# A triangular inverse that keeps its running matrix in PSUM, and a new static order around it

## The chip, the cores and the metric

One core of one Trainium2 chip runs the whole program. The metric is the device time of one execution in microseconds (us). All times below are in us unless marked ns. TensorE is called PE (its weight loads PEld), VectorE DVE, ScalarE ACT, GpSimd POOL, and SyncE, which issues most DMAs, SP.

## The reference

One layer of a hybrid decoder for two request groups that share weights: 1024 prompt tokens and 8 decode tokens. Each token passes a half-step SwiGLU network, a mixing layer and a second half-step SwiGLU network:

```python
h = x + 0.5 * rmsnorm(swiglu(rmsnorm(x, lp['n_ffn1_pre']), lp['ffn1_gate'], lp['ffn1_up'],
                             lp['ffn1_down']), lp['n_ffn1_post'])
u = rmsnorm(h, lp['n_mix_pre'])
proj = u @ lp['w_in']
...
mix = jnp.concatenate([ya, yb], axis=-1) @ lp['w_out']
h = h + rmsnorm(mix, lp['n_mix_post'])
h = h + 0.5 * rmsnorm(swiglu(rmsnorm(h, lp['n_ffn2_pre']), lp['ffn2_gate'], lp['ffn2_up'],
                             lp['ffn2_down']), lp['n_ffn2_post'])
```

`ya` is differential attention of 4 heads, `yb` an RWKV-7 recurrence of 8 heads with a 64 x 64 state each:

```python
def step(s, inp):
    r_t, w_t, k_t, v_t, kk_t, a_t = inp
    sa = jnp.einsum('nhvk,nhk->nhv', s, -kk_t)
    s = (s * w_t[:, :, None, :] + sa[..., None] * (kk_t * a_t)[:, :, None, :]
         + v_t[..., None] * k_t[:, :, None, :])
    return s, jnp.einsum('nhvk,nhk->nhv', s, r_t)
```

The kernel does this recurrence in chunks of 64 tokens. Inside a chunk it needs the inverse of a triangular matrix, and that inverse is what the change touches.

## The kernel before

**Halves and phases.** The tokens are cut into two halves of 512 (one carries the 8 decode tokens too). The two networks on two halves make four phases: phase 0 and 1 are the first network on half 0 and 1, phase 2 and 3 the second network. All their gate, up and down matmuls come from one stream, `s_trunk`, named `trunk`. Weights are loaded in full precision and split into two rounded parts (ACT rounds, DVE or POOL subtracts: `wts_w` for the trunk, `lin_w` for the projections), and each product takes three matmuls. Phases 1 and 2 use matmuls of 512 columns (wide) except for their last tiles; the others use 256 or 264 (narrow). A phase ends with its tail: norm, residual, and for phases 0 and 1 the normed input of the mixing projection (`tail_xl`, `tail_T`). The tail of phase 2 is named `last`, the end of phase 3 `end`.

**Mixing of one half.** `proj_m` computes the projection `w_in`. Four jobs (`s_job`, function `job`) do two RWKV heads each, jobs 0 and 2 on buffer set 0, jobs 1 and 3 on set 1. Attention (`attn`, with `prep` before and `fin` after each head) follows. Then `s_out` multiplies by `w_out`: `out_m` for half 0, `outb_m` for half 1, 384 matmuls each. Its norm is `s_outnorm`: one statistics matmul `outn_dec` per chunk of about 256 tokens, then additions on DVE and POOL into `out_T` or `outb_T`. After it `s_stats` and `s_pre` make the rounded input of the next network: `pre_X` for phase 2, `pre_T` for phase 3. The handover from mixing to the next network is this chain of matmul, norm, statistics and rounding. `rows` transposes half 1's residual for the output.

**One job.** It builds its operands on all engines, multiplies, and writes 32 x 32 blocks of a lower triangle to DRAM (`Md`). The inverse reads them back into `LT` (`job_LT` for set 0, `job_lraw` for set 1), laid out so that each of 128 partitions holds part of one block, and loads a starting block into `X`. Then 31 steps follow, each with two DVE instructions: a product of one row of `LT` with one column of `X` into `tm`, and an addition of `tm` onto the rest of `X`. Each needs the one before. `X` and `tm` lie in one SBUF tile, which the trace names `bset_solve` for set 0 and `job_hres` for set 1. The result goes through DRAM (`Xd`) into the matrix `TT`, and the job's later matmuls use it. A job has one PSUM bank, `aux0` or `aux1` (named `job_aux` in the trace), which `ps2()` hands out; during the inverse it is not used.

**What sets the order.** Every piece of work is a stream, a generator that hands its instructions to a queue per engine. `Kern.run` takes them one at a time, by a cost formula for each instruction (`price`), and fixes the order on each engine before the program runs; on the chip every engine executes its list in that order. [...] Of the instructions ready at about the same time the one with the smallest `late` goes first, a due time that the previous planning pass left for it (`latest`). `either` chooses between DVE and POOL (or ACT) for some instructions by what stands in their queues, so a new order also moves some work between engines. The program plans `PASSES` times and uses the pass whose own total is lowest.

Of the kernel before, what the change touches and what calls it, by code (L numbers as in the profile page):

```python
# [83 lines left out]
MW = 1  # L84
MARG = 0
SLACK = 0.02
PASSES = 10

PRIO = {"stats": (1, 1), "lin": (1, 1), "proj": (1, 1), "tail": (0, 0), "dec": (1, 1), "job": (-2, 0), "trunk": (-1, 3), "wts": (0, 0), "outb": (1, 1), "out": (0, 0), "resid": (-2, 0)}

# [93 lines left out]
class Kern:  # L184
# [97 lines left out]
    def put(self, eng, op, fn, a, k):  # L282
        st = self.cur
        outs = [a[0]] + ([k["accum_out"]] if "accum_out" in k else [])
        ins = [getattr(x, "ap", None) if isinstance(x, bass.IndirectOffsetOnAxis) else x for x in a[1:]]
        ins += [v for n, v in k.items() if n != "accum_out"]
        ins = [x for x in ins if isinstance(x, bass.AP)]
        i = len(self.ops)
        o = Op(eng, lambda: fn(*a, **k), st)  # L289

        o.key = st.key, st.count
        st.count += 1

        o.before = st.put.get(eng)
        st.put[eng] = i
        o.late = self.late.get(o.key) if self.late else None
        self.price(o, op, a, k, outs[0], ins)
        if op == "activation" and a[2] in TABLE:
            o.table = TABLE[a[2]]
        deps = set()  # L300
        for write, aps in ((False, ins), (True, outs)):
            for ap in aps:
                nm = ap.tensor.name
                if nm in self.tiles:
                    s, row = self.tiles[nm]
                    assert s.tenant == nm, (nm, s.tenant)
                    q, w = self.region(ap, s, row)
                    deps |= s.before
                    if ap.space == PSUM:

                        deps.update(j for (e, _), j in s.last.items() if e != eng)
                    s.last[eng, st] = i
                    deps.update(np.unique(s.wrote[q, w]).tolist())
                    if write:
                        for r in s.read.values():
                            deps.update(np.unique(r[q, w]).tolist())
                            r[q, w] = -1
                        s.wrote[q, w] = i
                    else:
                        if (eng, st) not in s.read:  # L320
                            s.read[eng, st] = np.full((4, s.words), -1, np.int64)
                        s.read[eng, st][q, w] = i
                elif nm in self.drams:
                    shape, seen = self.drams[nm]
                    box = self.box(ap, shape)
                    deps.update(j for b, w, j in seen if (write or w) and all(x[0] <= y[1] and y[0] <= x[1] for x, y in zip(b, box)))
                    seen.append((box, write, i))
        deps -= {-1, i}
        for j in deps:
            d = self.ops[j]  # L330
            if d.end is None:
                d.then.append(o)
                o.left += 1
            else:
                o.ready = max(o.ready, self.after(d, o))
        o.deps = deps
        self.ops.append(o)
        self.backlog[eng] += o.cost
        st.q[eng].append(o)
        st.n += 1  # L340
# [68 lines left out]
    def spawn(self, gen, label, prio, *banks, ahead=None):  # L409
        prio = PRIO.get(label.rstrip("01"), prio)  # L410
        self.streams.append(Stream(gen, label, prio, banks))
        k = self.spawned[label] = self.spawned.get(label, -1) + 1
        self.streams[-1].key = label, k
        if ahead is not None:
            self.streams[-1].ahead = ahead

# [358 lines left out]
    def s_weights(self):  # L775

        nc, I = self.nc, self.I
        groups, seq = self.plan()
        last, turn = {}, -1
        for ph in range(4):  # L780
            tags = ("w0", "w1", "w2", "w3")[:4 if ph in (0, 3) else 2]
            turn = -1
            for n, (kind, f, m0) in enumerate(seq):
                if ph == 1 and n == 2 * LEAD:
                    yield ("wait", ("loaded", ("in", 0), 25))
                    last |= {tag: ("used", ("in", 0), 24 + i) for i, tag in enumerate(tags)}
                turn += 1
                tag = tags[turn % len(tags)]
                if ph == 3 and turn == 2:
                    yield ("wait", ("outw", 1))  # L790
                raw = self.raw()
                w = I[f"ffn{1 + ph // 2}_{kind}"]
                if kind == "down":
                    grp = groups[f]
                    a = len(grp)
                    nm = self.down_tiles(grp) * P
                    raw = raw[:, :a * nm]
                    src = w[0, grp[0] * P:(grp[-1] + 1) * P, m0 * P:m0 * P + nm].rearrange("(q p) m -> p q m", p=P)
                else:
                    src, a = self.column(w, f), KT  # L800
                nc.sync.dma_start(raw.rearrange("p (a b) -> p a b", a=a), src)
                if tag in last:
                    yield ("wait", last[tag])
                self.W[ph, kind, f, m0] = self.split(raw, tag, a)
                self.signal(("loaded", ph, kind, f, m0))
                last[tag] = ("used", ph, kind, f, m0)
                yield

    def s_trunk(self):

        nc = self.nc
        V, A, G = nc.vector, nc.scalar, nc.gpsimd
        groups, _ = self.plan()
        for ph in range(4):
            if ph == 0:
                ring = self.T(self.big, [P, 4160], "xl1", FR)
            wide = ph in WIDE
# [543 lines left out]
    def job(self, pool, i, s, jb):  # L1361
# [3 lines left out]
        V, A, G = nc.vector, nc.scalar, nc.gpsimd  # L1365
# [5 lines left out]
        r, k, v = F("r"), F("k"), F("v")  # L1371
# [3 lines left out]
        ps = self.ps2()  # L1375
# [5 lines left out]
        ps = self.ps2()  # L1381
# [10 lines left out]
        ps = self.ps2()  # L1392
        for j in range(4):
            mm(ps[:, 2 * j:2 * j + 2], sq[:, j * P:(j + 1) * P], self.ind2, start=True, stop=True)
        rn, sx, st = (x[:, j] for x in [self.T(pool, [P, 3, 8], "stf")] for j in range(3))
# [7 lines left out]
        ps = self.ps2()  # L1403
# [12 lines left out]
        ps = self.ps2()  # L1416
# [33 lines left out]
        for w0 in (-1, 3, 7):  # L1450
            ps = self.ps2().rearrange("p (n h t) -> p n h t", n=4, h=2)
# [21 lines left out]
        for g in range(2):  # L1473
            for h, q in H:
                ps = self.ps2().rearrange("p (n w t) -> p n w t", n=4, w=2)
# [17 lines left out]
        for n in range(NC):  # L1493
            for h, q in H:
                o = H[1 - h][1]
# [10 lines left out]
        solve = [x[:, 256 * j:256 * j + 256] for j in range(2)]  # L1506
# [2 lines left out]
        for cg in range(4):  # L1509
            nc.sync.dma_start(LT[32 * cg:32 * cg + 32], src)  # L1510
        LT = LT.rearrange("p (s t) -> p s t", s=32)
        X, tm = (t.rearrange("p (c i) -> p c i", i=32) for t in solve)
        yield
        for j in range(31):
            w, m = 31 - j, j // 4 + 1
            V.tensor_tensor(tm[:, :m, :w], LT[:, j, j + 1:].unsqueeze(1).broadcast_to([P, m, w]),
                            X[:, :m, j:j + 1].broadcast_to([P, m, w]), ALU.mult)
            V.tensor_tensor(X[:, :m, j + 1:], X[:, :m, j + 1:], tm[:, :m, :w], ALU.add)
            if j % 2:
                yield  # L1520
        for cg in range(4):
            nc.sync.dma_start(self.Xd[jb][:, :, cg, :], X[32 * cg:32 * cg + 32])
        yield
# [9 lines left out]
        ps = self.ps2().rearrange("p (n t) -> p n t", t=C)  # L1533
# [7 lines left out]
        for g in range(2):  # L1541
            ps = self.ps2().rearrange("p (n h t) -> p n h t", n=4, h=2)
# [4 lines left out]
        ps = self.ps2().rearrange("p (n t) -> p n t", t=C)  # L1547
# [9 lines left out]
        for g in range(2):  # L1557
            ps = self.ps2().rearrange("p (n w t) -> p n w t", n=4, w=2)
# [11 lines left out]
        for g in range(2):  # L1570
            ps = self.ps2().rearrange("p (n w t) -> p n w t", n=4, w=2)
# [34 lines left out]
        st = J([P, 3, 8], "st")  # L1606
# [12 lines left out]
        ps = self.ps2()  # L1619
# [6 lines left out]
        ps = self.ps2()  # L1626
# [684 lines left out]
```

## Time and profile before

| | us |
|---|---|
| runs | 2412.41, 2413.09, 2421.26 (median 2413.09) |
| the profiled execution | 2414.15 |
| its span on the core | 2412.3 |
| from 2012 to 2412 (phase 3): PE busy | 392.68 |

The profile's page gives busy time by engine and 40 slices of the span, with the granted clock of PE in tenths. A group of instructions is a row: engine, operation, tile written and tiles read, shape, count, then busy us, mean ns of one, and the idle time of the engine just before them with what ended it. A row of a table by windows gives start and end, the length, then busy us and instructions of PE, PEld, DVE, ACT and POOL, the granted clock (1 is full), the DMA share and GB/s. Almost every row has line 289, since one helper issues all planned instructions; the tile names tell them apart. The DMA queues carry little that decides here:

```profile
q1 hardware_dynamic: 460824, 294.78, 42.5%
HBM read 254.86 MB, written 41.46 MB: 123 GB/s over the span
```

### The profile page before, as it was taken

What the parts mean: (1) busy time and instruction counts of PE and PEld (TensorE: products, weight loads), DVE (VectorE), ACT (ScalarE), POOL (GpSimd) and SP (SyncE); (2) the same over time, 40 slices, a digit from 0 to 9 for tenths busy, and PEclk for the clock granted to TensorE, in tenths of its full rate; (3) what the DMA queues carried; (4) which work ended last, traced back from release to release, by engine and by line L of the source; (5) the groups of instructions that cost most, each with busy time, mean ns of one, the idle gap of its engine ahead of it and who ended that gap; (6) DMA issues with size and microseconds to landing.
All of it is one profiled execution on the core that took longest, in us unless ns stands there. A gap on an engine that the chain in (4) does not pass through costs nothing. (4 is left out here: it accounts for less than half of the span.)

```text
span 2412.3 us, 42260 instructions
## 1 busy us (share of the span) xinstructions
PE 2306.1 (96%) x16207; PEld 2045.4 (85%) x16207; DVE 1504.6 (62%) x3057; ACT 1023.0 (42%) x2008; POOL 967.4 (40%) x767
## 2 busy tenths in 40 slices
PE   7999999999999999996899999999999987999998
PEld 6999999799977778786887776777777887999998
DVE  5554445756379778567786288586687577343444
ACT  5532223543432443366543442443466455322224
POOL 4442223533087443446574244243434365111112
PEclk9999999999999999998899999999999998999999
DMA  6423233345375345465686343233534544323232
GB/s 202 126 87 92 87 91 120 110 147 151 97 220 166 99 114 147 121 167 154 161 223 178 114 118 90 61 94 87 154 112 132 156 121 113 114 85 93 88 92 76
DMA packets 461635, 299.09 MB, mean 124 GB/s; under 512 B 81114, under 2 KB 428862, under 8 KB 461433
## 3 DMA queue, kind: packets, MB, share of 16 engines
q1 hardware_dynamic: 460824, 294.78, 42.5%
q8 instruction: 128, 2.10, 0.4%
q0 software_dynamic: 320, 1.08, 0.1%
q14 instruction: 75, 0.61, 0.1%
q10 hardware_dynamic: 288, 0.52, 0.1%
HBM read 254.86 MB, written 41.46 MB: 123 GB/s over the span
## 5 line engine op out<-in xcount | busy, mean ns | idle before, releaser
L289 PE MATMUL trunk_m<-pre_X,wts_w 128*128 128x256 f32 (+2 forms) x3264 | 545.9, 321 | 11.0 <-DVE trunk_g L289 4.4
L289 POOL TENSOR_TENSOR wts_w<-wts_raw,wts_w 128x1024 fp32r<-128x1024 f32 (+1 forms) x147 | 334.8, 2278 | 524.4 <-ACT wts_w L289 445.4
L289 PE MATMUL trunk_m<-trunk_xl,wts_w 128*128 128x256 f32 (+2 forms) x2952 | 508.4, 324 | 14.9 <-DVE trunk_xl L289 13.8
L289 PEld LDWEIGHTS trunk_m<-pre_X,wts_w 128*128 128x128 f32 x3264 | 455.1, 190 | 56.2 <-issue 7.5
L289 ACT CAST wts_w<-wts_raw 128x1024 fp32r<-128x1024 f32 (+1 forms) x288 | 281.3, 977 | 445.3 <-PE trunk_m L289 360.3
L289 PEld LDWEIGHTS trunk_m<-trunk_xl,wts_w 128*128 128x128 f32 x2952 | 420.4, 190 | 55.7 <-DVE trunk_xl L289 15.6
L289 PE MATMUL trunk_m<-pre_T,wts_w 128*128 128x256 f32 (+2 forms) x2592 | 445.7, 327 | 2.1 <-DVE wts_w L289 0.8
L289 PEld LDWEIGHTS trunk_m<-pre_T,wts_w 128*128 128x128 f32 x2592 | 375.7, 188 | 45.7 <-issue 3.7
L289 POOL TENSOR_TENSOR trunk_xl<-trunk_t,trunk_xl 128x256 fp32r<-128x256 f32 (+2 forms) x104 | 114.9, 1105 | 290.1 <-ACT trunk_xl L289 290.0
L289 DVE TENSOR_TENSOR trunk_xl<-trunk_xl,trunk_m 128x256 f32<-128x256 f32 (+2 forms) x314 | 155.8, 502 | 112.3 <-PE trunk_m L289 110.8
L289 DVE TENSOR_TENSOR wts_w<-wts_raw,wts_w 128x1024 fp32r<-128x1024 f32 (+1 forms) x141 | 162.5, 1153 | 65.3 <-ACT wts_w L289 62.8
L289 PE MATMUL proj_m<-tail_xl,lin_w 128*128 128x256 f32 (+1 forms) x832 | 159.9, 290 | 4.0 <-ACT tail_xl L289 4.0
L289 PE MATMUL proj_m<-tail_T,lin_w 128*128 128x512 f32 (+1 forms) x672 | 153.1, 384 | 0.1
L289 PEld LDWEIGHTS proj_m<-tail_T,lin_w 128*128 128x128 f32 x672 | 119.7, 190 | 26.6 <-issue 2.0
L289 PEld LDWEIGHTS proj_m<-tail_xl,lin_w 128*128 128x128 f32 x832 | 132.4, 192 | 7.4 <-ACT tail_xl L289 4.5
L289 PE MATMUL proj_m<-tail_X,lin_w 128*128 128x256 f32 (+1 forms) x416 | 121.9, 293 | 0.4 <-DVE tail_X L289 0.3
L289 ACT CAST trunk_xl<-trunk_t 128x256 fp32r<-128x256 f32 (+2 forms) x136 | 64.0, 471 | 127.2 <-DVE trunk_t L289 78.8
L289 DVE SCALAR_TENSOR_TENSOR trunk_g<-trunk_t,trunk_m 128x512 f32<-128x512 f32 (+2 forms) x78 | 43.4, 557 | 91.4 <-ACT trunk_t L289 90.8
L289 POOL TENSOR_TENSOR trunk_g<-trunk_g,init_rb 128x256 f32<-128x256 f32 (+1 forms) x44 | 42.0, 956 | 135.0 <-ACT trunk_t L289 135.0
L289 PE MATMUL trunk_aux<-pre_T,wts_w 128*128 128x264 f32 (+1 forms) x672 | 85.4, 283 | 0.0
L289 PEld LDWEIGHTS proj_m<-tail_X,lin_w 128*128 128x128 f32 x416 | 80.1, 193 | 3.9 <-issue 2.2
L289 PEld LDWEIGHTS trunk_aux<-pre_T,wts_w 128*128 128x128 f32 x672 | 82.4, 188 | 0.0
(498 smaller groups left out, 3610.7 us busy)
## 6 DMA issues: line engine op xcount, KB each, us to landing
wts_raw<-in_ffn_gate_dram SPq DMA_DIRECT2D x88, 512.0 KB
wts_raw<-in_ffn_up_dram SPq DMA_DIRECT2D x88, 512.0 KB
wts_raw<-in_ffn_down_dram SPq DMA_DIRECT2D x96, 384.0 KB
lin_raw<-in_w_in_dram SPq DMA_DIRECT2D x26, 512.0 KB
mix_T<-PT SPq DMA_DIRECT2D x37, 256.0 KB
wts_raw<-in_ffn_down_dram SPq DMA_DIRECT2D x16, 512.0 KB
dec_dreg<-in_cache_k_dram SPq DMA_DIRECT2D x32, 256.0 KB
dec_dreg<-in_cache_v_dram SPq DMA_DIRECT2D x32, 256.0 KB
```

The costliest lines, as they stand in the source:

```text
L289: o = Op(eng, lambda: fn(*a, **k), st)
```

## The change

The inverse now takes the job's own PSUM bank for `X`. ACT copies the starting block from SBUF into the bank (256 columns), the 31 steps read and write `X` there while `tm` and `LT` stay in SBUF, and ACT copies the result back, so that the DMA can read it. Each of the eight jobs has two more ACT copies. The arithmetic is the same.

The order is planned anew. A table `BIAS` adds microseconds to the due times of eight streams: negative numbers make a stream more urgent (the weights of phase 3, half 1's last job, the tail of phase 0's second chunk, the norm of half 0's first chunk), positive ones less (the residual load of phase 0, the second half's input, half 1's two norms). Streams get a name with a number for that (`part`), and the number of planning passes goes from 10 to 4.

```diff
@@ -84,7 +84,8 @@
 SLACK = 0.02
-PASSES = 10
+PASSES = 4
+BIAS = {"tail1": -10, "ldxb0": 10, "wts3": -30, "outn3": 3, "job13": -30, "outn2": 3, "resid0": 60, "outn0": -10}
@@ -294,6 +295,8 @@
         o.late = self.late.get(o.key) if self.late else None
+        if o.late is not None:
+            o.late += BIAS.get(st.part, 0)
         self.price(o, op, a, k, outs[0], ins)
@@ -411,6 +414,7 @@
         self.streams[-1].key = label, k
+        self.streams[-1].part = f"{label}{k}"
@@ -778,6 +782,7 @@
         for ph in range(4):
+            self.cur.part = f"wts{ph}"
@@ -812,6 +817,7 @@
         for ph in range(4):
+            self.cur.part = f"trunk{ph}"
@@ -1509,7 +1515,10 @@
         LT = LT.rearrange("p (s t) -> p s t", s=32)
-        X, tm = (t.rearrange("p (c i) -> p c i", i=32) for t in solve)
+        cols = lambda t: t.rearrange("p (c i) -> p c i", i=32)
+        ps = self.ps2()
+        X, tm = cols(ps[:, :256]), cols(solve[1])
+        A.copy(ps[:, :256], solve[0])
         yield
         for j in range(31):
             w, m = 31 - j, j // 4 + 1
@@ -1518,6 +1527,8 @@
             V.tensor_tensor(X[:, :m, j + 1:], X[:, :m, j + 1:], tm[:, :m, :w], ALU.add)
             if j % 2:
                 yield
+        A.copy(solve[0], ps[:, :256])
+        X, tm = (cols(t) for t in solve)
         for cg in range(4):
```

**The inverse on DVE.** The first job's inverse begins so in the list of DVE before (`bset_solve` is `X` and `tm` in SBUF):

```order
L289 TENSOR_TENSOR mix_T_580_5265<-mix_T_580_5265,mix_T_581_5266 128x512
L289 TENSOR_TENSOR bset_solve_181<-job_LT_5921,bset_solve_181 128x31
L289 TENSOR_TENSOR bset_solve_181<-bset_solve_181 128x31
L289 TENSOR_TENSOR bset_solve_181<-job_LT_5921,bset_solve_181 128x30
L289 TENSOR_TENSOR bset_solve_181<-bset_solve_181 128x30
```

And now:

```order
L290 TENSOR_TENSOR mix_T_580_5287<-mix_T_580_5287,mix_T_581_5288 128x512
L290 TENSOR_TENSOR bset_solve_181<-job_LT_5870,job_aux_641_5871 128x31
L290 TENSOR_TENSOR job_aux_641_5871<-job_aux_641_5871,bset_solve_181 128x31
L290 TENSOR_TENSOR bset_solve_181<-job_LT_5870,job_aux_641_5871 128x30
L290 TENSOR_TENSOR job_aux_641_5871<-job_aux_641_5871,bset_solve_181 128x30
```

Each product reads `X` from the bank `job_aux`, each addition reads and writes it there; one SBUF input is left in both.

**The first handover on PE** (half 0's norm, `outn_dec`, after the last `out_m`). Before, phase 1's trunk is finished, and the next half's projection follows:

```order
L289 MATMUL out_m_1337_12650<-out_X_1250_11596,lin_w_1319_12522 128x256 x2
L289 MATMUL out_m_1337_12650<-out_X_1251_11597,lin_w_1319_12522 128x256
L289 MATMUL out_m_1337_12650<-out_X_1250_11596,lin_w_1319_12522 128x256
L289 MATMUL proj_m_1367_12714<-tail_T_1296_11849,lin_w_1363_12710 128x256
L289 MATMUL outn_dec_12622<-bset_la_173,init_onesD_76 128x256
L289 MATMUL proj_m_1367_12714<-tail_T_1297_11850,lin_w_1363_12710 128x256
```

Now (`decb` is work of the decode tokens):

```order
L290 MATMUL trunk_m_1233_11509<-trunk_xl_56_153,wts_w_1227_11468 128x512 x3
L290 MATMUL decb_dec_10963<-decb_dreg_10961,bset_wa_166 128x8 x4
L290 MATMUL trunk_m_1233_11509<-trunk_xl_56_153,wts_w_1227_11468 128x512 x2
L290 MATMUL outn_dec_11971<-bset_la_173,init_onesD_76 128x256
L290 MATMUL trunk_m_1233_11509<-trunk_xl_56_153,wts_w_1227_11468 128x512 x4
L290 MATMUL trunk_m_1234_11529<-trunk_xl_56_153,wts_w_1227_11468 128x512 x9
L290 MATMUL trunk_m_1237_11547<-pre_T_132_513,wts_w_1231_11500 128x512
```

Phase 1's trunk, gates still among it, now stands on both sides of the norm, and phase 1's tail and the next projection come after it.

**The second handover on PE** (half 1's second `outn_dec`). Before, phase 2's trunk surrounds it:

```order
L289 MATMUL trunk_m_2151_19515<-trunk_xl_56_153,wts_w_2133_19370 128x256 x5
L289 MATMUL outn_dec_19626<-bset_sg_174,init_onesD_76 128x256
L289 MATMUL trunk_m_2151_19515<-trunk_xl_56_153,wts_w_2133_19370 128x256 x4
L289 MATMUL rows_cb_19366<-init_ident_69,outb_T_2034_18540 128x128
L289 MATMUL trunk_m_2154_19567<-trunk_xl_56_153,wts_w_2133_19370 128x256 x8
L289 MATMUL rows_cb_19367<-init_ident_69,outb_T_2035_18541 128x128 x4
```

Now it stands behind the last `outb_m`, and what follows is phase 3:

```order
L290 MATMUL outb_m_2203_19893<-outb_T_2081_18914,lin_w_2201_19839 128x256
L290 MATMUL rows_cb_19596<-init_ident_69,outb_T_2089_18922 128x128 x3
L290 MATMUL rows_cb_19597<-init_ident_69,outb_T_2088_18921 128x128 x4
L290 MATMUL stats_dec_19593<-bset_bv_80_177,init_onesD_76 128x264
L290 MATMUL rows_cb_19598<-init_ident_69,outb_T_2089_18922 128x128 x4
L290 MATMUL outn_dec_19918<-bset_sg_174,init_onesD_76 128x256
L290 MATMUL trunk_m_2248_19974<-pre_T_2225_19951,wts_w_2133_19186 128x264
```

The trunk of phase 2 has moved ahead of `outb_m`; of the 252 trunk matmuls that stood among its 384, 26 are left.

## The prediction

> **What bounds the kernel now.** I read the page first, then busy time by stage, then the waits of PE, and last the groups of the job's inverse. The page:
>
> ```profile
> span 2412.3 us, 42260 instructions
> PE 2306.1 (96%) x16207; PEld 2045.4 (85%) x16207; DVE 1504.6 (62%) x3057; ACT 1023.0 (42%) x2008; POOL 967.4 (40%) x767
> PE   7999999999999999996899999999999987999998
> PEclk9999999999999999998899999999999998999999
> ```
>
> TensorE is the bound: only 106 us of the span is not PE work, so no edit can win more than that and what a lowered clock costs. The change adds no matmul and removes none; what it can move is where PE stands idle. The stretches by stage (us; PE, PEld, DVE, ACT, POOL busy; PEclk, DMA):
>
> ```profile
> 500.00:1120.00 620.00, 606.40 (x4140) 509.85 (x4139) 436.61 (x1036) 253.57 (x534) 286.03 (x200) 0.99 0.51 145
> 1120.00:1180.00 60.00, 37.09 (x232) 32.85 (x231) 55.26 (x94) 37.74 (x80) 38.93 (x40) 0.72 0.50 138
> 1372.00:1700.00 328.00, 320.32 (x2146) 246.76 (x2145) 231.92 (x559) 138.86 (x280) 120.90 (x81) 0.99 0.33 90
> 1700.00:1900.00 200.00, 193.27 (x1065) 158.03 (x1064) 149.34 (x335) 114.29 (x281) 84.61 (x51) 1.00 0.48 137
> 1900.00:2012.00 112.00, 91.03 (x684) 86.13 (x683) 72.59 (x102) 63.00 (x118) 59.11 (x57) 0.91 0.39 115
> ```
>
> The long job and attention stretches lose little: 13.6 us in half 0 (500 to 1120), 14.4 us in half 1 (1372 to 1900). The two places where one stage hands over to the next lose 22.9 us and 21.0 us. Closer:
>
> ```profile
> 1120.00:1140.00 20.00, 7.81 (x50) 6.40 (x48) 19.59 (x35) 14.77 (x29) 12.97 (x13) 0.75 0.22 66
> 1140.00:1160.00 20.00, 9.28 (x31) 6.57 (x31) 19.52 (x36) 10.84 (x22) 16.00 (x19) 0.50 0.51 159
> 1160.00:1180.00 20.00, 20.00 (x152) 19.88 (x152) 16.16 (x26) 12.13 (x29) 9.96 (x10) 0.90 0.76 188
> 1180.00:1200.00 20.00, 20.00 (x172) 20.00 (x171) 14.32 (x19) 10.65 (x24) 10.30 (x11) 1.00 0.45 128
> 1972.00:1992.00 20.00, 14.30 (x93) 12.36 (x92) 17.04 (x27) 12.77 (x28) 14.67 (x17) 0.83 0.37 106
> 1992.00:2012.00 20.00, 5.99 (x38) 5.08 (x37) 12.68 (x24) 10.29 (x22) 8.80 (x12) 0.66 0.00 0
> ```
>
> From 1120 to 1160 DVE is busy 39.1 of 40 us and PE 17.1. Then the granted clock is down: 31 matmuls took 9.28 us at 0.50, where 0.12 us each (row below) would be 3.7, so 5.6 are lost; 1160 to 1180 holds 20 matmuls fewer than the next 20 us, 2.4 more; at 0.75 some 1.5. First handover: 22.9 + 9.5 = 32 us. The second loses 19.7 us between 1972 and 2012, and its 131 matmuls took 20.3 us where 0.12 each would be 15.7: 24.
>
> ```profile
> PE trunk_m L289 <- DVE trunk_xl L289: 14.1, 4, 12.5
> PE fin_cb L289 <- POOL mix_T L289: 8.8, 1, 8.8
> PE job_dec L289 <- DVE mix_T L289: 5.2, 2, 3.3
> PE job_aux L289 <- DVE bset_solve L289: 1.5, 1, 1.5
> ```
>
> No long wait of PE is on the inverse itself. It acts through DVE time and through the length of the job chain.
>
> **The inverse on DVE.** Eight jobs, 62 instructions each, alternately a product into `tm` and an addition into `X`:
>
> ```profile
> L289 DVE TENSOR_TENSOR job_hres<-job_lraw,job_hres 128x60 f32<-128x60 f32 (+24 forms) x124 | 60.6, 489 | 1.8
> L289 DVE TENSOR_TENSOR bset_solve<-job_LT,bset_solve 128x60 f32<-128x60 f32 (+24 forms) x124 | 45.5, 367 | 5.9 <-DMA job_LT<-Md 3.6
> L289 DVE TENSOR_TENSOR job_hres<-job_hres 128x60 f32<-128x60 f32 (+24 forms) x124 | 44.5, 359 | 2.0
> L289 DVE TENSOR_TENSOR bset_solve<-bset_solve 128x60 f32<-128x60 f32 (+25 forms) x126 | 38.2, 303 | 2.6
> L289 DVE TENSOR_TENSOR job_hres<-job_lraw,job_hres x124: 161/218/2449, 713.6 to 1653.0; 128x60 f32<-128x60 f32 x12, 128x28 f32<-128x28 f32 x8, 128x54 f32<-128x54 f32 x8, 128x48 f32<-128x48 f32 x8
> L289 DVE TENSOR_TENSOR mix_T<-mix_T 128x512 f32<-128x512 f32 x24 | 25.6, 1065 | 2.0 <-ACT mix_T L289 1.8
> L289 DVE TENSOR_TENSOR mix_T<-mix_T,job_dec 128x512 f32<-128x512 f32 x16 | 10.9, 684 | 9.2 <-PE job_dec L289 9.2
> L289 POOL TENSOR_TENSOR wts_w<-wts_raw,wts_w 128x1024 fp32r<-128x1024 f32 x108 | 262.2, 2428 | 403.0 <-ACT wts_w L289 352.2 <-issue 27.3 <-DVE bset_Sd L289 7.5
> L289 DVE TENSOR_TENSOR wts_w<-wts_raw,wts_w 128x1024 fp32r<-128x1024 f32 (+1 forms) x141 | 162.5, 1153 | 65.3 <-ACT wts_w L289 62.8 <-DMA dec_dreg<-Qd 2.1
> L289 DVE STREAM_TRANSPOSE bset_solve<-bset_TT x8: 425/434/436, 600.4 to 1635.5; 32x256 f32<-32x256 f32 x8
> ```
>
> The median is 218 ns, the longest 2449 ns, about one POOL subtraction (2428). Of two groups of 512-wide instructions of this kind, the one with both inputs in SBUF averages 1065 ns, the one with an input in PSUM 684. So an operand in PSUM spares DVE the waits for POOL. With `X` in PSUM both instructions of a step have one SBUF input. At the median, 496 x 0.217 = 107.6 us instead of 188.8: **81 us of DVE time go**. Half 0 alone (the same windows for the tile of set 0, then of set 1; PE, PEld, DVE, ACT):
>
> ```profile
> 500.00:1120.00 620.00, 3.25 (x128) 2.58 (x128) 43.96 (x128) 1.46 (x4) 0.99 0.51 145
> 500.00:1120.00 620.00, 3.25 (x128) 2.58 (x128) 63.56 (x128) 1.46 (x4) 0.99 0.51 145
> ```
>
> Half 0 has 107.5 us, with 8 transposes of 0.43 us off, 104; it falls by 50, half 1 by the other 31.
>
> What no row shows is a DVE write into PSUM. Reads are free (groups between 500 and 1700 us):
>
> ```profile
> L289 DVE TENSOR_SCALAR job_stf<-job_stf 128x8 f32<-128x8 f32 x8 | 1.3, 164 | 0.0
> L289 DVE TENSOR_SCALAR job_stf<-job_dec 128x8 f32<-128x8 f32 x8 | 1.3, 162 | 8.6 <-PE job_dec L289 8.6
> L289 DVE TENSOR_TENSOR trunk_xl<-trunk_xl,trunk_m 128x512 f32<-128x512 f32 x73 | 49.8, 683 | 22.9 <-PE trunk_m L289 22.2
> L289 DVE TENSOR_TENSOR trunk_xl<-trunk_xl,trunk_m 128x256 f32<-128x256 f32 x16 | 6.7, 417 | 4.2 <-PE trunk_m L289 3.9
> ```
>
> 162 against 164 ns. Two widths give 266 ns per 256 columns, so a fixed part of 150 ns. Bounds for an addition that writes PSUM: nothing, and the fixed part once more, 124 x 0.15 = 18.6 us a half. I take nothing, since the read is free.
>
> [...]
>
> The two copies a job on ACT, 16 in all:
>
> ```profile
> L289 ACT COPY out_T<-out_m 128x256 f32<-128x256 f32 x16 | 5.9, 371 | 14.3 <-PE out_m L289 14.3
> ```
>
> That is 5.9 us in all on an engine 42% busy: nothing on PE's path, while each job's chain grows by 0.74 us and two handovers. If ACT had no room there, it would be 6 us. The copy in also makes ACT wait for the DMA of the starting block where DVE did. Behind it on ACT stand the evacuation of a `proj_m` tile in the first job, of trunk tiles and weight casts in the second, and PE waits for those banks and weights. DVE's waits for the block loaded beside it come to 3.6 us in all (the `job_LT<-Md` above). Bounds 0 to 6; I take 0, with ACT idle for more than half of the span.
>
> **The new order, first handover.** Before, half 0's `out_m` (384 matmuls) starts when phase 1's trunk is finished, and nothing else covers its norm and the trunk's tail. Now trunk matmuls stand behind the first `out_m`: 173 of 512 columns and 240 of 256. Their pitch, from the chain of waits (start, us, what):
>
> ```profile
> 1586.56 12.08 PE trunk_m L289 x52
> 2059.39 5.75 PE trunk_m L289 x48
> ```
>
> 0.232 and 0.120 us: 40.1 + 28.8 = 69 us of cover that came earlier before; between half 0's last `proj_m` and the first `out_m` the trunk goes from 1272 wide and 242 narrow (324 us) to 1099 wide and none (255 us). From the first `outn_dec` to the tail's last statistic the new PE list holds 128 wide and 338 narrow trunk matmuls, phase 2's first gates among them: 29.7 + 40.6 = 70 us. DVE has there what it did from 1120 to 1180, 55.3 us, and the trunk's own: 16 additions of 0.417, 10 gate steps of that shape or twice it, about 0.45, 6 weight subtractions of 1.15, 18 in all. 74 against 70: 4 us of PE idling, and 4 more for waits in order. **32 - 8 = 24 us gained**; bounds 10 (DVE alone sets the pace, as now) and 32.
>
> **What pays for it.** The 69 us were cover for half 0's jobs and attention. Their chain must now get 69 us shorter or PE stalls there. It has the 50 us of the inverse and 18 us of trunk work that DVE no longer does in it: 68. I charge 4 us for misfit, a third of the 13.6 idle now; bounds -5 and +54. Half 1, from its last `proj_m` to its last `attn`, goes from 1296 wide and 41 narrow (306 us) to 1152 and 209 (292 us): 13 us of cover less against 31 us of DVE work. I take 4 of its 14.4 idle us; bounds 0 and -14.
>
> **Second handover.** Before, phase 2's last trunk matmuls lie behind it, and PE waits 12.5 us for one trunk addition queued on DVE behind phase 3's `pre_T`. Now only 26 trunk matmuls stand among the `outb_m`, where 252 stood, and after the last `outb_m` stand norm, statistics and two sets of `pre_T` in a row. The list on DVE from `outn` to the last `pre_T` is nearly the one that took from 1973 to 2007; PE has 72 gate and up matmuls and transposes to put in, where it had 131 matmuls. I take **0**; bounds -10 and +10, the latter if `outb_m`, now without trunk between, waits for its weights.
>
> **Sum.** -24 + 4 - 4 + 0 + 0 = -24 us. The profiled execution took 2414.15 us (span 2412.3); 2414 - 24 = 2390. The median shown is 2413.09, 1 us lower, so the forecast stands as 2390, -1.0%.
>
> **Rivals.** *The stretches give too* (0.20): half 1 gives its 14, half 0 nothing lost, second handover -10: 24 + 14 + 10 = 48, 2366. For it: DVE was the busiest engine beside PE at both handovers. Against: PE idles only 28 us in the job stretches.
> *Writes into PSUM cost the fixed part again* (0.12): 18.6 us a half. In half 0 they come straight onto the missing cover, in half 1 they eat the 4: -24 + 4 + 18.6 + 0 = -1, about 2413, no change. Against: the reads. [...]
> *Half 0's chain does not shorten* (0.16): it is set by its DRAM round trips and by other DVE work, not by the inverse, and PE, with 69 us of cover gone, stands before the job's matmuls. Only the 18 us of trunk work leave the chain, so 69 - 18 = 51 more, less 24: +27, 2441. It decides from a chain that shortens by less than 45 us. For it: PE's longest waits in half 0's jobs, 5.2 us, are for `mix_T` and not for the inverse (1.5). Against: DVE is busy 437 of 620 us there.
>
> **Numbers.** The forecast has 0.52, its own range 2370 to 2405. Under 2355 I leave 0.05, above 2425 0.14. This kernel's time tells a change of about 0.5% (12 us) from none. Faster than 2401: 0.47 of the forecast and the first rival, 0.67; within: 0.05 and the second, 0.17; slower: 0.16.
>
> **What would show it.** The inverse's instructions near 217 ns with none over 1 us; PE idle and a lowered clock gone around `out_m`, the `outn_dec` of half 0 amid trunk matmuls; no new long wait of PE on `job_aux`; still some 20 us idle before phase 3. Phase 3 itself stays 400 us, so its start tells the result. It is wrong if the additions take 300 ns or more, or if PE's idle time between 500 us and the first `out_m` grows by more than 24 us.

## The result and the profile after

| | us |
|---|---|
| the changed kernel, median of 13 | 2426.02 (2422.74 to 2430.77) |
| the kernel before, median of 13 | 2413.37 (2401.7 to 2421.26) |
| ratio | 1.0056, 95% interval 1.0042 to 1.007 |
| span of the profiled execution | 2423.3 (before 2412.3) |

The change makes the kernel slower by 0.56%, some 13 us. The page of the changed kernel:

```profile
span 2423.3 us, 42273 instructions
PE 2316.6 (96%) x16207; PEld 2052.6 (85%) x16207; DVE 1414.5 (58%) x3078; ACT 1023.9 (42%) x2015; POOL 931.4 (38%) x751
PE   7999999999999999999699999999999888999998
```

DVE has 90 us less to do (1504.6 before), POOL 36 us less, and PE is idle for as long as it was (2423.3 - 2316.6 = 106.7 us, 106.2 before). So the work was saved and the time was not. The bubble of PE that stood in slices 19 and 20 is in slice 20 now, and the second one, slices 33 and 34 before, has become three slices, 32 to 34.

The inverse itself, in the groups of DVE:

```profile
L290 DVE TENSOR_TENSOR job_aux<-job_aux,bset_solve 128x60 f32<-128x60 f32 (+24 forms) x124 | 26.7, 215 | 2.5
L290 DVE TENSOR_TENSOR job_aux<-job_aux,job_hres 128x60 f32<-128x60 f32 (+24 forms) x124 | 26.7, 215 | 2.5
L290 DVE TENSOR_TENSOR bset_solve<-job_LT,job_aux 128x60 f32<-128x60 f32 (+24 forms) x124 | 25.4, 205 | 5.7 <-DMA job_LT<-Md 2.8
L290 DVE TENSOR_TENSOR job_hres<-job_lraw,job_aux 128x60 f32<-128x60 f32 (+24 forms) x124 | 25.4, 204 | 4.2 <-DMA job_lraw<-Md 1.9
L290 DVE TENSOR_TENSOR job_aux<-job_aux,bset_solve x62: 160/218/245, 553.9 to 811.3; 128x60 f32<-128x60 f32 x6, 128x28 f32<-128x28 f32 x4, 128x54 f32<-128x54 f32 x4, 128x48 f32<-128x48 f32 x4
```

The four groups make 104.2 us where they made 188.8, and in the last row (set 0, half 0; shortest, median and longest in ns) no addition takes more than 245 ns. Of the same 62 the longest took 2428 before, and of the products of set 1, the row in the prediction, 2449.

To see where the time went I use one measure for all kernels, the **loss of PE**: for each matmul in the trace the time until the next one starts, less what a matmul of that shape usually takes to the next (the median of the lower 60% of its kind in the trace of before), summed over a stretch. It holds idle time and lowered clock together. The stretches have the same bounds for all kernels, although the work in them shifts: half 1's first `outb_m` starts at 1879 before and at 1918 in the changed kernel, half 0's first `out_m` at 1129 and at 1048.

| stretch (us) | what lies there | before | after | difference |
|---|---|---|---|---|
| 0 to 480 | phase 0, start | 39.8 | 40.9 | +1.1 |
| 480 to 1120 | half 0's jobs and attention | 83.5 | 78.7 | -4.8 |
| 1120 to 1240 | first handover | 38.1 | 37.0 | -1.1 |
| 1240 to 1920 | half 1's projection, jobs, attention | 95.3 | 86.6 | -8.7 |
| 1920 to 2040 | `outb_m`, second handover | 30.5 | 56.9 | +26.4 |
| 2040 to the end | phase 3 | 7.4 | 6.0 | -1.4 |

The sum is +11.5; the spans differ by 11.0. The second handover costs more than all the rest gives. Counted by the work and not by the clock, PE loses 22.9 us between the first `outb_m` and the last, where it lost 3.3 before. It is there in the windows (columns as in the prediction):

```profile
1920.00:2000.00 80.00, 62.90 (x453) 58.58 (x451) 55.02 (x76) 45.00 (x81) 35.68 (x36) 0.89 0.69 198
2000.00:2040.00 40.00, 30.17 (x115) 21.89 (x114) 25.35 (x39) 21.35 (x41) 18.78 (x23) 0.67 0.10 26
```

From 1920 to 2000, where `outb_m` runs almost alone, PE stands idle for 17 us and does 453 matmuls. The waits of PE between 1900 and 2030, and the chain of waits at the start of `outb_m`:

```profile
PE rows_cb L290 <- ACT rows_X L290: 5.2, 5, 1.8
PE outb_m L290 <- ACT outb_T L290: 4.9, 1, 4.9
PE trunk_m L290 <- ACT pre_T L290: 3.6, 4, 2.0
PE fin_cb L290 <- POOL mix_T L290: 2.7, 1, 2.7
PE outb_m L290 <- DVE lin_w L290: 2.6, 3, 1.9
```

```profile
1926.60 1.72 DMA YM<-init_E
1928.38 2.93 DMA outb_hres<-YM
1931.33 0.63 ACT outb_T L290
1931.98 0.70 DVE outb_T L290
1932.73 4.12 PE outb_m L290 x17
...
1958.03 4.92 DMA lin_LT<-in_w_out_dram
1963.03 1.06 ACT lin_w L290
1964.11 1.22 DVE lin_w L290
```

The last head's result goes to DRAM and back, is rounded, and only then can `outb_m` use it: 6.1 us from the write's start to the first matmul. After that each piece of `w_out` is a transfer, a cast and a subtraction of 7.2 us together. All of this was there before too; there trunk matmuls ran beside it. Now no single wait is long, but there are many.

At the first handover the window of before and that of the changed kernel stand almost alike:

```profile
1120.00:1240.00 120.00, 96.02 (x636) 86.89 (x635) 99.94 (x145) 66.57 (x137) 74.66 (x72) 0.86 0.64 170
```

```profile
1120.00:1240.00 120.00, 99.47 (x547) 86.63 (x547) 97.46 (x143) 66.37 (x125) 83.11 (x86) 0.87 0.48 144
...
1180.00:1200.00 20.00, 8.61 (x33) 6.86 (x33) 18.06 (x26) 10.17 (x22) 16.69 (x21) 0.66 0.41 129
```

PE is idle there for 24 us before and for 20.5 after, at the same clock, and the bubble, now between 1180 and 1200, is as deep as the one from 1140 to 1160 was. Only what PE waits for has changed (waits of PE, 1100 to 1230):

```profile
PE trunk_m L290 <- DVE pre_X L290: 12.2, 5, 5.4
PE trunk_m L290 <- POOL wts_w L290: 3.4, 1, 3.4
```

Phase 2's first gates wait for `pre_X`, their own input, which the handover makes.

Half 0's chain did get shorter. Its `out_m` stand 81 us earlier (shortest, median, longest in ns, then the start of the first and the last; first before, then in the changed kernel):

```profile
L289 PE MATMUL out_m<-out_X,lin_w x384: 277/281/583, 1128.5 to 1204.8; 128*128 128x256 f32 x192
L290 PE MATMUL out_m<-out_X,lin_w x384: 277/280/287, 1048.2 to 1141.7; 128*128 128x256 f32 x192
```

### The profile page after: what moved, and what is told of

It is laid out like the page before. It is cut to its first block, busy times and chain, and to the rows that moved or that the text cites. A ratio compares the mean times of both kernels' runs of the same rounds, so it can differ in the third digit from the quotient of the medians.

```text
span 2423.3 us, 42273 instructions
## 1 busy us (share of the span) xinstructions
PE 2316.6 (96%) x16207; PEld 2052.6 (85%) x16207; DVE 1414.5 (58%) x3078; ACT 1023.9 (42%) x2015; POOL 931.4 (38%) x751
## 4 chain that ended last, share of the span: by engine, by line
PE 80%; DVE 8%; DMA 5%; ACT 3%; issue 2%; POOL 1%; SPq 1%; DVEq 0%; ACTq 0%; POOLq 0%
PE trunk_m L290 49%; PE proj_m L290 12%; PE job_aux L290 6%; PE trunk_aux L290 5%; PE out_m L290 2%; PE attn_m L290 2%; PE attn_aux L290 1%; SPq L290 1%; PE job_dec L290 1%; DVE mix_T L290 1%; DMA decb_dreg<-Dd 1%; DVE pre_X L290 1%; PE outb_m L290 1%; DMA mix_T<-PT 1%; DMA bset_sg<-PT 1%
## 5 line engine op out<-in xcount | busy, mean ns | idle before, releaser
L290 PE MATMUL trunk_m<-pre_X,wts_w 128*128 128x256 f32 (+2 forms) x3264 | 551.7, 325 | 25.0 <-DVE pre_X L290 13.9
L290 PEld LDWEIGHTS trunk_m<-pre_X,wts_w 128*128 128x128 f32 x3264 | 467.6, 194 | 68.2 <-DVE pre_X L290 15.6
L290 POOL TENSOR_TENSOR wts_w<-wts_raw,wts_w 128x1024 fp32r<-128x1024 f32 (+1 forms) x137 | 315.3, 2302 | 511.5 <-ACT wts_w L290 447.1
L290 PE MATMUL trunk_m<-trunk_xl,wts_w 128*128 128x256 f32 (+2 forms) x2952 | 503.3, 323 | 6.7 <-DVE trunk_xl L290 4.3
L290 PE MATMUL trunk_m<-pre_T,wts_w 128*128 128x256 f32 (+2 forms) x2592 | 465.4, 332 | 11.0 <-DVE wts_w L290 4.7
L290 DVE TENSOR_TENSOR wts_w<-wts_raw,wts_w 128x1024 fp32r<-128x1024 f32 (+1 forms) x151 | 172.7, 1144 | 122.8 <-ACT wts_w L290 122.3
L290 POOL TENSOR_TENSOR trunk_xl<-trunk_t,trunk_xl 128x256 fp32r<-128x256 f32 (+2 forms) x103 | 115.4, 1120 | 282.9 <-ACT trunk_xl L290 275.5
L290 PE MATMUL proj_m<-tail_T,lin_w 128*128 128x512 f32 (+1 forms) x672 | 146.9, 378 | 0.0
L290 DVE TENSOR_TENSOR trunk_t<-trunk_g,trunk_m 128x512 f32<-128x512 f32 (+2 forms) x78 | 43.5, 558 | 63.3 <-PE trunk_m L290 56.4
```

## The experiments

In all of them a ratio is the kernel's time to that of the kernel before, run beside it, with its 95% interval.

### The two parts of the change, and the move apart from the order

The change moves `X` and plans a new order at once. The expectations of these runs set three theories against each other. The one named Cover: the move saves time at a given order, but a plan made with the shorter inverse runs phase 2's trunk earlier, and none is left beside `outb_m`; for e1 it gave 2420 to 2445 us.

Two runs plan each part alone. The first:

```diff
-PASSES = 4
-BIAS = {"tail1": -10, "ldxb0": 10, "wts3": -30, "outn3": 3, "job13": -30, "outn2": 3, "resid0": 60, "outn0": -10}
+PASSES = 10
+BIAS = {}
```

> X in PSUM as in the change, but no table of biases and ten planning passes as before. [...] Move (the copies and handovers in each job's chain cost more than the shorter additions give, at any order): 2420 to 2430. Due times (the biases or the fewer passes cost it): 2413 or less.

The second keeps the table and the four passes:

```diff
-        ps = self.ps2()
-        X, tm = cols(ps[:, :256]), cols(solve[1])
-        A.copy(ps[:, :256], solve[0])
+        X, tm = cols(solve[0]), cols(solve[1])
...
-        A.copy(solve[0], ps[:, :256])
-        X, tm = (cols(t) for t in solve)
```

> The biases and four passes of the change, X in SBUF as before. Cover: 246 trunk matmuls stand among the outb_m as before, so 2400 to 2420 us. Move: 2400 to 2415. Due times: 2426 or more, with PE idle around outb_m as in the changed kernel.

Two more hold the order fixed. The program plans with `X` in one place and notes every pick; it then builds with `X` in the other place and takes the instructions in the noted order (the copies on ACT are put in, or left out, where they become ready):

```diff
+        for m in more:
+            if o is None or o.left or when(m) <= when(o):
+                return when(m), m
+        self.at += 1
+        return when(o), o
...
+    X_PSUM, LOOSE, SCRIPT = not X_PSUM, True, b[3]
+    nc = build(b[2], False)
```

> The order of before, instruction by instruction on PE, DVE, POOL and SP, with X in PSUM and the two copies a job put in on ACT. Cover: the inverse falls from 189 to 108 us of DVE time and nothing is moved away from outb_m, so 2395 to 2408 us. Move: 2420 to 2430. Due times: 2413 or a little less.

> The order of the changed kernel with X in SBUF and without the copies. Cover: the inverse is back near 189 us of DVE time, in an order that stands on the short one, and outb_m is as uncovered: 2435 to 2470 us. Move: the copies and handovers are gone: 2410 to 2420, faster than the change. Due times: 2426.

| | order | X | median us | ratio |
|---|---|---|---|---|
| e1 | planned with X in PSUM, no table | PSUM | 2466.49 | 1.0215 [1.0181, 1.025] |
| e2 | planned with X in SBUF and the table | SBUF | 2429.68 | 1.0064 [1.0044, 1.0084] |
| e3 | that of before | PSUM | 2404.66 | 0.9957 [0.9938, 0.9977] |
| e4 | that of the changed kernel | SBUF | 2521.12 | 1.044 [1.0397, 1.0484] |

**In the old order the move saves time**: e3 is 0.43% faster than before. So the theory that the move itself costs falls: copies, handovers and all, it gives. Its inverse takes what it takes in the changed kernel (here the additions of set 0 in the groups of e3), and half 1 loses less; the loss from 1240 to 1920 goes from 95.3 to 87.6, all else stays within 1.2:

```profile
L294 DVE TENSOR_TENSOR job_aux<-job_aux,bset_solve 128x60 f32<-128x60 f32 (+24 forms) x124 | 26.7, 215 | 2.5
1372.00:1700.00 328.00, 324.19 (x2173) 250.09 (x2173) 202.60 (x575) 142.63 (x290) 123.29 (x82) 1.00 0.34 92
```

DVE was busy for 231.9 us of that window before, PE for 320.3. One wait of PE for the inverse's tile stood there, in the waits of before from 1430 to 1490, and is gone in e3:

```profile
PE job_dec L289 <- DVE job_hres L289: 4.2, 1, 4.2
```

**The new order cannot do without it.** e4 is 95 us slower than the changed kernel, more than was expected of any theory. Its inverse is back at 184 us (one group of it below), and the loss is 125.6 us in half 0 and 135.4 from 1240 to 1920, where the changed kernel has 78.7 and 86.6 (e4's `outb_m` starts only at 2008, so the second stretch does not hold quite the same work):

```profile
L294 DVE TENSOR_TENSOR bset_solve<-bset_solve 128x60 f32<-128x60 f32 (+25 forms) x126 | 48.8, 387 | 2.5
```

**Each part planned alone loses.** e1 has no trunk matmul among its `outb_m`; it was expected slow for that, and is slower still: its `outb_m` starts only at 1949, and from 1920 to 2080 it loses 73 us (32 before, 57 in the changed kernel), after 93 in half 0. e2 speaks against the cover theory as I had put it: 246 trunk matmuls do stand among its `outb_m`, and up to 2000 the stretch loses 10.0 us where the changed kernel loses 29.6. But half 0 loses 96.3 us, 12.8 more than before, and so it is slower all the same. The theory that the table alone is at fault falls with e1. What remains is that the order of before is a good one among many: the three kernels planned anew so far (the change, e1, e2) are slower by 13, 53 and 16 us, for reasons of which only some were followed, and the move alone is faster by 9.

### Is it the missing cover beside outb_m?

The loss at the second handover was put down to the trunk that no longer stands beside `outb_m`. Two runs test it from both sides. The first gives cover back to the changed kernel: its order is kept up to half 1's first `proj_m`, and from there phase 2's trunk is less urgent.

```diff
+    UPTO = next(n for n, i in enumerate(SCRIPT[0]) if i in b[4])
+    BIAS = {**BIAS, "trunk2": 300, "wts2": 300}
     nc = build(b[2], False)
```

> The changed kernel's order up to half 1's first proj_m; from there phase 2's trunk and its weights are planned as less urgent by 300 us, so that 188 trunk matmuls instead of 26 stand among the outb_m. Cover decides (the second handover is long because no trunk is left beside outb_m): the 57 us that PE loses from 1920 to 2040 us fall to about 35, and the time to 2400 to 2410 us. Only moved (what outb_m gets, half 1's jobs and attention lose): the handover is shorter by some 20 us, the stretch before it longer by as much, 2420 to 2430.

The second takes it from the old order, with `X` in PSUM as in e3:

```diff
+    at = [n for n, i in enumerate(picks) if i in outb]
+    between = [i for i in picks[at[0]:at[-1]] if i in trunk]
+    LATER = set(between[24:]), picks[at[-1]]
```

> The old order with X in PSUM, but of the 252 trunk matmuls that stand among the outb_m 228 may go only after the last outb_m (24 stay); everything else keeps its order as far as it can. 92 wide and 136 narrow ones, 92 x 0.231 + 136 x 0.117 = 37 us of cover, go from beside outb_m to behind it. Cover decides (outb_m cannot be kept going from its weights and the last head's result alone): PE loses 15 to 30 us more up to the last outb_m, and the time is 2420 to 2440 us. It does not (the trunk covers norm and rounding behind outb_m as well as it covered outb_m): 2400 to 2410.

g1 takes 2434.45 us, ratio 1.0096 [1.0076, 1.0117], 30 us more than e3 with nothing changed but the place of 228 trunk matmuls and of the instructions that hang on them. Between 1840 and 2040 the loss goes from 33.7 to 64.8 us; between the first `outb_m` and the last it goes from 3.2 to 25.3, and the other 9 us are lost behind. One window and the waits of PE (1830 to 2040) of g1:

```profile
1840.00:2040.00 200.00, 155.84 (x985) 137.45 (x985) 102.61 (x165) 92.25 (x171) 81.45 (x74) 0.88 0.35 101
PE trunk_m L296 <- DVE trunk_xl L296: 16.9, 2, 16.6
PE outb_m L296 <- DVE lin_w L296: 6.9, 5, 4.6
PE outb_m L296 <- ACT outb_T L296: 4.8, 1, 4.8
```

and the same window and waits of e3:

```profile
1840.00:2040.00 200.00, 178.90 (x1237) 164.30 (x1237) 130.74 (x207) 107.26 (x197) 99.34 (x91) 0.95 0.46 132
PE trunk_m L294 <- DVE trunk_xl L294: 13.9, 3, 12.5
PE outb_m L294 <- DVE outb_T L294: 1.1, 1, 1.1
```

Without trunk between, `outb_m` waits for its weights and for the last head's result, 11.7 us in place of 1.1; in the changed kernel these are the same two waits, 7.5 us. And the trunk behind it covers little there: its own last addition still stands on DVE behind norm and rounding, and PE waits 16.6 us for it. So the cover is what `outb_m` lives on: in the old order this is shown, and the changed kernel, with 26 trunk matmuls there and 22.9 us of loss, fits it.

e5 takes 2443.78, ratio 1.0138 [1.0114, 1.0162], 18 us more than the changed kernel and slower than either theory expected. Beside `outb_m` the cover does what it should: from 1920 to 2000 the loss falls from 29.6 to 10.4 us. But from 2000 to 2040 it loses 31.1 (27.3 in the changed kernel), and its last `outb_m` stands at 1982, where the changed kernel's stands at 1993; from 1240 to 1920 the loss is 107.2 instead of 86.6. The windows of e5, the start of half 1's jobs, `outb_m`, and behind it:

```profile
1400.00:1520.00 120.00, 106.11 (x600) 78.57 (x599) 89.72 (x222) 51.46 (x91) 46.36 (x32) 0.87 0.70 154
1920.00:2000.00 80.00, 73.89 (x599) 72.37 (x598) 50.08 (x65) 46.87 (x88) 39.40 (x36) 0.96 0.51 149
2000.00:2040.00 40.00, 19.72 (x103) 15.03 (x102) 27.98 (x46) 20.75 (x40) 21.02 (x26) 0.65 0.17 45
```

Only moved, then, and at a loss: what `outb_m` got, the stretch before it lacks. By the end of half 1's projection the changed kernel has spent trunk of phase 2 that the old order still has: 98 wide and 310 narrow trunk matmuls stand between `out_m` and the projection, phase 2's gates among them, and 166 wide ones amid it. In the old order 55 narrow ones stand in the projection and none between `out_m` and it. e5 can hold back only what comes after the first `proj_m`. The projection needs no cover there: in the time line of the changed kernel 260 of its matmuls follow one another at 0.233 us each.

```profile
1269.76 60.61 PE L290 MATMUL proj_m<-tail_T,lin_w 128*128 128x512 f32 x260
```

### The first handover: who sets its length?

Phase 2's gates wait there for `pre_X`, 16 DVE instructions of 13.6 us. Two runs take this work away in the changed kernel's order: the first shrinks it, the second leaves it out.

```diff
+                if ph == 2 and SKIP:
+                    self.x[ph] = [(h, h) for h, _ in x]
+                    x = [(h, [t[:, :8] for t in l]) for h, l in x]
```

> The changed kernel's order, with the second rounded part of phase 2's input left out: the 16 instructions on DVE that write pre_X shrink to 8 columns, and phase 2's matmuls read the first part twice. DVE decides the first handover (phase 2's gates wait there for pre_X behind norm, tail and statistics on one queue): about 12 us of DVE work go between 1165 and 1210, and the time falls by 8 to 13, to 2413 to 2418 us. Latencies decide (the hops from statistics to norm to rounding, not DVE's work): less than 4 us, 2422 to 2426.

```diff
+                    self.gone = SKIP and ph == 2 and part == 1
                     step()
...
-            if self.dry:
+            if self.dry or o.gone:
                 continue
```

> As the run with the shrunken residue, but its 16 instructions on DVE are not there at all (phase 2's input has its first rounded part alone, read twice). They took 13.6 us between 1165 and 1210 in the changed kernel and still 8.6 us at 8 columns. DVE's queue decides the first handover: PE's loss there falls from 34 to about 22 us, and the time to 2412 to 2417 us. The chain of hops decides: 2422 to 2426.

2425.66 us (ratio 1.0058 [1.0041, 1.0076]) and 2424.54 (1.0053 [1.0034, 1.0072]): nothing is won that can be told from none. The loss from 1120 to 1240 is 37.0 in the changed kernel, 34.6 and 32.6 here. So the work on `pre_X` does not decide it alone, and my theory falls. The waits of PE in e9, 1150 to 1230, show what stands there in its place, and the window in the middle of them how busy DVE is:

```profile
PE tail_aux L298 <- DVE init_rb L298: 5.0, 1, 5.0
PE stats_dec L298 <- POOL bset_bv L298: 3.9, 1, 3.9
PE trunk_m L298 <- POOL wts_w L298: 3.4, 1, 3.4
1180.00:1200.00 20.00, 8.57 (x32) 6.50 (x32) 19.02 (x29) 10.20 (x23) 16.22 (x20) 0.61 0.40 132
```

The waits for DVE's part of `pre_X` are gone, and behind them stand those for phase 1's tail and for the statistics of half 0's result. It looks as if two chains end at the same place, and with one shorter PE waits for the other. DVE is still busy for 19.0 of 20 us there, with the work of tail and statistics, so how much of the wait is DVE's time and how much the hops between engines stays open. Whether more independent matmuls there would close the gap was not tried.

### What can the inverse be worth at most?

Two runs in the old order with `X` in SBUF: each instruction of the inverse on one column, and the inverse's instructions left out.

```diff
-            w, m = 31 - j, j // 4 + 1
+            w, m = (1, 1) if SHORT else (31 - j, j // 4 + 1)
```

> The order of before with X in SBUF, but each of the inverse's instructions works on one column of one block: what the inverse can be worth at most in that order. Little waits for it (PE is covered by trunk in the job stretches): 2395 to 2405 us, at most 8 below the 2404.7 of the old order with X in PSUM. The job chain is the bound: half of the 190 us of additions and products show up, 2340 to 2380.

```diff
+            self.gone = NONE
             V.tensor_tensor(tm[:, :m, :w], LT[:, j, j + 1:].unsqueeze(1).broadcast_to([P, m, w]),
...
+            self.gone = False
```

> The order of before with the inverse's 496 instructions on DVE left out altogether (the starting block goes on as the result). In the run with one column each, which had X in SBUF, they still took 149 us, since most of them waited for POOL, so that run bounded little. Little in the old order waits for the inverse: 2392 to 2404 us, at most 12 below the old order with X in PSUM, although another 104 us of DVE time go. The job chain is the bound: 2340 to 2380.

2399.63 us (0.9949 [0.9932, 0.9967]) and 2391.92 (0.9922 [0.9904, 0.994]). The first bounds little, since one column still takes DVE 149 us in place of 189 (two of its groups, and the shortest, median and longest of another):

```profile
L294 DVE TENSOR_TENSOR job_hres<-job_hres 128x1 f32<-128x1 f32 x124 | 45.3, 365 | 2.0
L294 DVE TENSOR_TENSOR bset_solve<-job_LT,bset_solve 128x1 f32<-128x1 f32 x124 | 30.8, 249 | 4.5 <-DMA job_LT<-Md 2.0
L294 DVE TENSOR_TENSOR bset_solve<-bset_solve x126: 144/159/2341, 69.4 to 1614.3; 128x1 f32<-128x1 f32 x124, 1x128 f32<-1x128 f32 x1, 1x1 f32<-1x1 f32 x1
```

It is not so that most of them waited for POOL, as the second expectation says: half took 159 ns or less, and a few long ones make the mean. The second run bounds it: all 189 us of the inverse on DVE are worth 0.78%, some 19 us, in the old order. `X` in PSUM gets 0.43% out of these 0.78%. The rest of the 189 us does not show in the time.

This bound is for the old order alone, which has 376 other DVE instructions between the steps of the eight inverses. From a job's first product to the end of its last, added up over the eight jobs, the inverse takes 395 us before and 382 in e3 and in e8, however fast its own instructions are. In the changed kernel, with 267 others between, it takes 214. So the new order did shorten the inverse as a chain, by 181 us, and still lost. The next run, f0, has 185 there and is no faster than e3.

### A better order?

The last two plan anew, but from the old order: up to 500 us it is kept, and from there the due times come from e3's order with the shorter inverse in it. The second adds a table of its own.

```diff
+    UPTO = next(n for n, i in enumerate(b[3][0]) if b[4][i] >= 500)
+    BIAS = MORE
     nc = build(late, False)
```

`MORE` is empty in the first run, and in the second `{"attn10": -30, "decb0": -30, "lin1": -10, "trunk2": 60, "attn11": -60, "outb0": -30}`.

> X in PSUM, no biases; up to 500 us the order of before, from there planned with due times that were worked out from the old order with the shorter inverse in it. The order keeps out_m behind phase 1's trunk and 251 trunk matmuls among the outb_m. The order decides: as good as the old order with X in PSUM, 2395 to 2408 us. Any planning anew with X in PSUM loses: 2420 or more.

> As the run before it, with biases that make half 1's attention, outb_m and the decode tokens' work more urgent and phase 2's trunk less (60 us). Between half 1's last proj_m and its first outb_m stand 1219 wide trunk matmuls where the old order has 1300, so outb_m starts sooner; 163 wide ones are left among the outb_m. The order decides: 2380 to 2398 us, faster than the old order with X in PSUM by 6 or more. Only moved (what outb_m and the handover behind it gain, the jobs lose): 2400 to 2412.

f0 takes 2404.3 us (0.9963 [0.9945, 0.998]), f1 2406.9 (0.9977 [0.9961, 0.9994]). Both are faster than before and than the change, and no better than e3. In f1 the second handover loses 21.1 us where e3 loses 30.7, as meant, but half 0 loses 94.8 for 82.4; f0 has 92.1 there, so most of this came with planning anew and not with the second table. Planning anew with `X` in PSUM need not lose. Both orders keep `out_m` behind phase 1's trunk and leave trunk among `outb_m`, 251 and 163; which of the two counts was not tested alone. e3, with 2404.66, is a version that beats both kernels, and f0 equals it.

## Why the prediction was wrong

**The inverse on DVE: right.** 81 us were to go, 84.6 went (188.8 - 104.2). Writes into PSUM cost little extra if anything: 215 ns for the additions, which write there, 205 for the products, which do not. The rival that they cost the fixed part once more falls. Rows of 8 columns show the same: the last addition of a job takes 0.17 us in PSUM in the changed kernel and 0.18 in SBUF in e4.

**The copies on ACT: right.** e3 holds them and is faster than before.

**What pays for the lost cover: inside its bounds.** Half 0 was charged 4 us, bounds -5 and +54; it won 4.8. Half 1 was to give 4, bounds 0 and -14; it gave 8.7 with its projection. e3 gives 7.7 there in the old order, so the shorter inverse can be the whole of it; in the new order it was not separated. The rival of the slower side, that half 0's chain does not shorten, gave the right sign for the wrong reason: `out_m` starts 81 us earlier, and half 0 lost nothing.

**First handover, -24: wrong.** The step "74 against 70: 4 us of PE idling" failed. The 70 us of cover were 128 wide and 338 narrow trunk matmuls between the first `outn_dec` and the tail's last statistic. I had seen that phase 2's first gates were among them and counted them all the same. In the list of PE 67 of the wide and 96 of the narrow ones read `pre_X`: 67 x 0.232 + 96 x 0.120 = 27 us of "cover" that waits for the very chain it was to hide. That leaves 43, and 74 - 43 = 31 us of loss; from 1160 to 1240 it is 34.3. That these two meet is partly luck. The 74 was too small as well: from the first `outn_dec` to the tail's last statistic, 1124 to 1230.6 us, DVE was busy for 87.7. And e9, without the waits for DVE's part of `pre_X`, still loses 32.6 from 1120 to 1240. So it is shown that the 70 us did not cover the chain, and that 1.1 us were won of 24; what sets the length of the bubble stays open.

**Second handover, 0: wrong, and this turned the sign.** It cost 26.4 us. The bound of +10 was a guess at a wait for weights. I had seen that 26 trunk matmuls were left of 252 and took from it only what would stand behind `outb_m`; the part beside it lost 22.9 us by itself, 19.6 more than before. g1 takes the same cover away in the old order, with the trunk put behind `outb_m` and not ahead of it as in the change: +30 us, 22 of them beside `outb_m`. At their pitches the 228 matmuls are about 37 us of cover, so four fifths of it came back as time.

**The sum.** Predicted: -24 + 4 - 4 + 0 = -24. Measured as loss, in the same order of terms: -1.1 - 4.8 - 8.7 + 26.4, with +1.1 and -1.4 at the two ends, 11.5. The expected gain was to come from the new order at the first handover and not from the inverse's time as such; it did not come, and the same order spent phase 2's trunk early, which cost the second handover. In the old order even the whole of the inverse's time on DVE is worth only 19 us (e10).

**What stays open.** What sets the length of the first handover, as said. Why the orders planned anew lose where they lose was followed only for the second handover. Which of the eight due times of the table does what was not tried one by one.

## What to carry to other kernels

Where an edit sets off a new plan, run the edit in the old order and the new order without the edit, before either is judged: here the edit gave 9 us in the old order, and the new order with the edit in it took 21. The two do not add: in the new order the edit is worth 95 us (e4). Matmuls that hide a chain are cover only if they do not read what the chain makes, and they can be spent once: count for every bubble which independent work is left at that point, and where it was spent. Time saved on an engine that PE does not wait for buys, in a given order, about as much at most as that order without the work at all, and this can be measured by leaving the work out: here 9 us (e3) of 19 (e10).

## What the runs showed of the hardware

In these runs a DVE instruction with two inputs in SBUF took long beside POOL however little it did. The inverse on one column (e8) still took 149 us, its four groups averaging 249 to 365 ns, with a median of 159 and, in the row above, a longest of 2341. What its 496 instructions took beyond that median makes 70 us; before, beyond a median of 217, it was 81. In e7 the 16 instructions on `pre_X` fell from 256 columns to 8 and from 13.6 to 8.6 us, 562 ns each. That the long ones wait for POOL is in the trace of before: 71 of the inverse's 496 took over 400 ns, and each of them ended within 0.1 us after a POOL instruction did. The longest, of 2449 ns, began at 768.91 us, a POOL subtraction of 2.71 us at 768.55. With one of the two inputs in PSUM none of the inverse's additions in the changed kernel's row takes over 245 ns, where the longest before took 2428. Of the inverse's instructions there, 277 began while one of POOL's ran, and 250 ended before it did; before, 2 of 89. So smaller instructions saved here their own work but hardly the waits (70 us in e8 for 81), and one input in PSUM saved the waits.
